# Copies of queries and keys as transfers within SBUF, group scaling on ScalarE, and a deeper early-load pipeline in a two-layer trunk

## The chip, the cores and the metric

The kernel runs on one core of one Trainium2 chip. The metric is the device time of one execution in microseconds (us). Below, PE is the matrix engine, DVE the vector engine, ACT the scalar (activation) engine, POOL the GpSimd engine and SP the engine that here issues almost all DMAs. SBUF is the on-chip working memory of 128 partitions, PSUM the accumulators that PE writes.

## The reference

One batch of 512 tokens with 1024 features goes through two layers, each of the form `x <- x + RMSNorm(mixer(RMSNorm(x)))`. The first layer holds 16 state-space (SSD) heads in 4 groups beside 16 forgetting-attention (FoX) heads; the second is a causal convolution module, which the change does not touch. All is float32. Cut to what matters for the change:

```
u = rmsnorm(x, g_pre);  proj = u @ w_in                       # 7200 columns: z, xBC, dt, q, k, v, f
yg = (y * silu(z_ssd)).reshape(b, s, SSD_GROUPS, 256)
yg = yg * rsqrt(mean(yg * yg, axis=-1) + EPS)                 # one scale per token and group
o: logits = (q . k) * 64**-0.5 + c_t - c_s, causal;  o = softmax(logits) @ v   # 16 heads of 64
out = concat([y, o]) @ w_out
x1 = x + rmsnorm(out, g_post);  then the convolution layer with its own o_w_in and o_w_out
```

## The kernel before, in words

Every large product is made of three PE matmuls on rounded parts: a float32 tensor is split into a high part (a rounded cast, mostly on ACT) and a low part (the difference, on DVE or POOL), and high x high, high x low and low x high are summed in PSUM. So every weight tile that is loaded (512 KB, L163) needs a cast (ACT, L157 or L159) and a subtraction (DVE or POOL, L191).

**Order of the work.** The program is a list of jobs (a weight tile and the matmuls on it), run one after the other. Between the matmuls of the first layer's jobs a small planner (`Steps`) puts the steps of the SSD groups and of the attention heads, each due a set modelled time after the steps that it needs: scores of a head (`sa`) are due 9 modelled us after its queries and keys (`("q", h), 9` and `("k", h), 9`). PE's order is thereby fixed in the program. On DVE, ACT, POOL and SP a scheduler puts the instructions in an order of its own when the program is built; on the chip each of these engines runs its list strictly in order, so an instruction that waits holds back all behind it.

**SSD groups.** For each of 4 groups, `gate` multiplies y by the gate, `gate_sums` takes the sums of squares (ACT, L358) and a power (POOL, L351), `gate_scale` (L1431) scales the four token blocks of 128 x 256, and `to_yT` transposes them on PE. PE transposes the next group's convolved inputs (`x_tokens`, tile `xt`) once their SiLU has run on ACT (tile `cv`, L95), and these need three convolution taps on DVE (L533).

**Queries and keys.** `qk_proj` makes two heads per pair of jobs. For each head the tile QS holds the rounded queries in partitions 0 to 63 (ACT, L610) and their low part in 64 to 127 (DVE, L611); QX repeats the rounded queries in 0 to 63 (L612) and has four rows of ones and cumulated gates below (POOL L613, DMA L614). KS holds the rounded keys (ACT, L623) twice (L625), KX their low part (DVE, L624) and four rows likewise (L626, L627). One score block is then two matmuls, KS x QS and KX x QX.

**Early low parts.** The second layer's weights are large, and DVE is full there. So `lo_ahead` makes the low parts of 52 of its weight tiles while the first layer runs: `load` (L202, 512 KB) brings a tile into SBUF, `sub` casts it into a scratch tile `prh` (ACT, L211, two halves) and subtracts that in place (DVE, L212, two halves), `store` writes the low part to DRAM (L216), from where the second layer fetches it. One step of this generator is taken every 7 or 8 pieces of the job list. In `run` and in the step order of `lo_ahead` a tile's subtraction comes two steps after its load.

Of the kernel before, what the change touches and what calls it, by code (L numbers as in the profile page):

```python
# [9 lines left out]
F32R = mybir.dt.float32r  # L10
BF16 = mybir.dt.bfloat16
AF = mybir.ActivationFunctionType
ALU = mybir.AluOpType
AX = mybir.AxisListType

P = 128
S = 512
# [19 lines left out]
def trunk(  # L37
# [6 lines left out]
    nc = tc.nc  # L44
    V, G, A, T = nc.vector, nc.gpsimd, nc.scalar, nc.tensor
# [2 lines left out]

    cp = ctx.enter_context(tc.tile_pool(name="const", bufs=1))
    rp = ctx.enter_context(tc.tile_pool(name="raw", bufs=3))  # L50
    ep = ctx.enter_context(tc.tile_pool(name="early", bufs=3))
    eh = ctx.enter_context(tc.tile_pool(name="earlyh", bufs=1))
    qp = ctx.enter_context(tc.tile_pool(name="q", bufs=7))
    tp = ctx.enter_context(tc.tile_pool(name="t", bufs=54))
    hp = ctx.enter_context(tc.tile_pool(name="spill", bufs=8, space=bass.MemoryType.DRAM))
    lop = ctx.enter_context(tc.tile_pool(name="los", bufs=64, space=bass.MemoryType.DRAM))
    sp = ctx.enter_context(tc.tile_pool(name="small", bufs=8))
# [11 lines left out]
    def nm(s):  # L69
        uid[0] += 1  # L70
        return f"{s}_{uid[0]}"

    def t2(s, dt=F32):
        return tp.tile([P, S], dt, tag="t", name=nm(s))
# [10 lines left out]
    def f32(t):  # L85
        return t.bitcast(F32)
# [108 lines left out]
    def lo_ahead(js):  # L195


        def load(j):
            w, r0, nk, c0, n = j.spec
            t = ep.tile([P, 1024], F32, tag="e", name=nm("pre"))  # L200
            with tc.issue_after(last_load[0]):
                nc.sync.dma_start(t.rearrange("p (k f) -> p k f", k=nk),  # L202
                                  w[r0 : r0 + nk * P, c0 : c0 + n].rearrange("(k p) f -> p k f", p=P))
            return t

        def sub(t):
            h = eh.tile([P, 1024], F32R, tag="eh", name=nm("prh"))
            for i in range(2):
                sl = slice(i * S, i * S + S)
                with tc.issue_after(last_cast[0]):  # L210
                    A.copy(h[:, sl], t[:, sl])  # L211
                V.tensor_tensor(t.bitcast(F32R)[:, sl], t[:, sl], f32(h)[:, sl], ALU.subtract)  # L212

        def store(j, t):
            j.lo = lop.tile([P, 1024], F32, tag="lo", name=nm("lo"))
            nc.sync.dma_start(j.lo, t)  # L216
        loaded = []
        for i in range(len(js) + 2):
            if i > 1:
                sub(loaded[i - 2])  # L220
            if i > 2:
                store(js[i - 3], loaded[i - 3])
            if i < len(js):
                loaded.append(load(js[i]))
            yield
        store(js[-1], loaded[-1])
# [47 lines left out]
    early = iter(())  # L274
# [243 lines left out]
    def fm_job(w, c0, evac, uh, ul, eng=None):  # L518
        def go(wh, wl):
            pb = bank("m")  # L520
            yield from fm_chunks(pb, P, wh, wl, uh, ul)
            evac(pb)
        return Job(w, 0, KT, c0, P, go, eng)
# [80 lines left out]
    def qk_proj(j):  # L604
        def evac_q(pq):
            for s in range(2):
                h = 2 * j + s
                src = slice(64 * s, 64 * s + 64)
                QS, QX = t2("QS", F32R), t2("QX", F32R)
                A.mul(QS[0:64, :], pq[src, :], 0.125)  # L610
                V.scalar_tensor_tensor(QS[64:128, :], pq[src, :], 0.125, f32(QS)[0:64, :], ALU.mult, ALU.subtract)  # L611
                V.tensor_copy(QX[0:64, :], f32(QS)[0:64, :])  # L612
                G.memset(f32(QX)[64:68, :], 1.0)  # L613
                nc.sync.dma_start(f32(QX)[66:68, :], f32(chl)[32 + h : 33 + h, :, :])  # L614
                qk["q", h] = (QS, QX)
                done["q", h] = now[0]

        def evac_k(pk):
            for s in range(2):
                h = 2 * j + s  # L620
                src = slice(64 * s, 64 * s + 64)
                KS, KX = t2("KS", F32R), t2("KX", F32R)
                A.copy(KS[0:64, :], pk[src, :])  # L623
                V.tensor_tensor(KX[0:64, :], pk[src, :], f32(KS)[0:64, :], ALU.subtract)  # L624
                V.tensor_copy(KS[64:128, :], f32(KS)[0:64, :])  # L625
                G.memset(f32(KX)[64:68, :], 1.0)  # L626
                nc.sync.dma_start(f32(KX)[64:66, :], f32(chl)[64 + h : 65 + h, :, :])  # L627
                qk["k", h] = (KS, KX)
                done["k", h] = now[0]
        fm_job(e_w_in, C_Q + j * P, evac_q, uh, ul)  # L630
        fm_job(e_w_in, C_K + j * P, evac_k, uh, ul)
# [624 lines left out]
    def q256(t, c):  # L1256
        return t[c // 2][:, c % 2 * 256 : c % 2 * 256 + 256]
# [169 lines left out]
    def gate_scale(g):  # L1427
        with tc.high_priority(offset=HP):
            y, r = SG[g]["y"], SG[g]["r"]
            for c in range(NB):  # L1430
                V.tensor_scalar(q256(y, c), q256(y, c), r[:, c : c + 1], None, ALU.mult)  # L1431

    def to_yT(g, f):
        y = SG[g]["y"]
# [14 lines left out]
    def ssd(steps):  # L1449
        add = steps.add  # L1450
        add("tk", decay_chain, ("dt", 24))
        for g in range(4):
# [29 lines left out]
            add(("gate", g), lambda g=g: gate(g), (("ya", 4 * g + 3), 0), (("yo", g), 0), (("silu", g // 2), 0), pe=False)  # L1482
            add(("gq", g), lambda g=g: gate_sums(g), (("gate", g), DL[9]), pe=False)
            add(("gs", g), lambda g=g: gate_scale(g), (("gq", g), DL[10]), pe=False)
            for f in range(2):
                add(("yT", g, f), lambda g=g, f=f: to_yT(g, f), *([(("yT", g, 0), 0)] if f else [(("gs", g), DL[11])]))
# [72 lines left out]
    for j in jobs[6:40]:  # L1559
        j.eng = G  # L1560
    early = lo_ahead([j for j in jobs[J1:JO1] + jobs[JO1 + 4 : JO1 + 8] if not j.make])
    run(1)
    steps = Steps()
# [30 lines left out]
    for half in range(2):  # L1594
        sl = slice(half * 256, half * 256 + 256)
# [51 lines left out]
```

## Time and profile before

| | us |
|---|---|
| median of 3 runs (927.5 to 927.8) | 927.53 |
| profiled execution, its own time | 929.48 |
| its span, first to last instruction | 927.6 |
| PE busy | 892.8 (96%) |
| DVE busy | 740.6 (80%) |
| ACT busy | 604.5 (65%) |
| POOL busy | 520.6 (56%) |

All rows are of the profiled execution. "Idle before" is the time for which the engine did nothing ahead of an instruction, with the instruction that ended that wait. The first layer fills the span up to about 570 us, the second the rest. SP, which only issues DMAs, has no busy time in these views.

### The profile page before, as it was taken

Reading aid. Unit: us, or ns where it says so; the run is one execution under the profiler, and the core shown is the slowest. Engines: PE = TensorE matmul, PEld = TensorE weight load, DVE = VectorE, ACT = ScalarE, POOL = GpSimd, SP = SyncE. Lnnn points to the kernel's source line nnn. Section 1 sums busy time; section 2 is a strip of 40 time slices with the busy share of each in tenths; the row PEclk is TensorE's granted clock in tenths of the full one; section 3 lists DMA queues with packets and bytes.
Section 4 is the critical chain, followed back from the end, with each engine's and each line's share of the span. In section 5 each row is a group of like instructions: output and inputs, shape, how many; then the busy total and the mean of one; then the engine's idle time right before and its main releaser. Section 6 shows DMA issues by size and latency. Waiting matters only on the chain.

```text
span 927.6 us, 13837 instructions
## 1 busy us (share of the span) xinstructions
PE 892.8 (96%) x4603; PEld 748.1 (81%) x4603; DVE 740.6 (80%) x1318; ACT 604.5 (65%) x1143; POOL 520.6 (56%) x478
## 2 busy tenths in 40 slices
PE   6999999997999999989899999999999999999997
PEld 6888788886888888778678889888888887787885
DVE  5667979888888897988888437899999999979502
ACT  5767567566856676577686437788785968658300
POOL 2733665554543444335573202998999999847410
PEclk9999999998999999999999999999999999999999
DMA  6736523348764675664648993655664655544503
GB/s 208 231 105 209 154 69 91 91 125 254 235 212 153 192 242 160 195 215 150 215 157 285 341 344 106 199 161 180 201 208 136 214 194 160 166 153 155 185 1 113
DMA packets 182506, 166.12 MB, mean 179 GB/s; under 512 B 7900, under 2 KB 151908, under 8 KB 182436
## 3 DMA queue, kind: packets, MB, share of 16 engines
q1 hardware_dynamic: 182420, 165.25, 55.6%
q8 instruction: 36, 0.59, 0.3%
q14 instruction: 34, 0.28, 0.1%
q10 hardware_dynamic: 16, 0.00, 0.0%
HBM read 133.64 MB, written 31.46 MB: 178 GB/s over the span
## 4 chain that ended last, share of the span: by engine, by line
PE 64%; DVE 14%; ACT 7%; issue 6%; DMA 4%; POOL 3%; SPq 0%; DVEq 0%; POOLq 0%; ACTq 0%
PE m L102 37%; PE o L102 18%; PE tm L102 4%; DVE pre L212 3%; POOL w L191 2%; ACT w L159 1%; DMA lo<-pre 1%; DMA pre<-in_o_w_in_dram 1%; PE s L102 1%; PE pT L106 1%; DVE cv L533 1%; DVE y L1431 1%; DVE seg L1380 1%; DVE pl L119 1%; DVE w L191 1%
## 5 line engine op out<-in xcount | busy, mean ns | idle before, releaser
L102 PE MATMUL m<-uh,w 128*128 128x512 f32 (+1 forms) x1392 | 452.9, 392 | 1.7 <-ACT yT L1441 1.0
L102 PEld LDWEIGHTS m<-uh,w 128*128 128x128 f32 x1392 | 261.9, 190 | 50.7 <-ACT yT L1441 1.4
L102 PE MATMUL m<-ul,w 128*128 128x512 f32 (+1 forms) x696 | 268.0, 385 | 0.0
L191 POOL TENSOR_TENSOR w<-wr,w 128x512 fp32r<-128x512 f32 x112 | 168.1, 1526 | 148.3 <-ACT w L159 112.3
L989 DVE SCALAR_TENSOR_TENSOR acc<-h,cw,acc 128x490 f32<-128x490 f32 (+13 forms) x274 | 178.9, 727 | 2.7 <-ACT acc L981 2.0
L896 POOL TENSOR_TENSOR acc<-acc,prod 128x507 f32<-128x507 f32 (+9 forms) x124 | 159.6, 1289 | 8.2 <-ACT prod L882 0.7
L102 PEld LDWEIGHTS m<-ul,w 128*128 128x128 f32 x696 | 132.4, 190 | 21.8 <-issue 0.5
L102 PE MATMUL o<-w,hlh 128*128 128x512 f32 x448 | 140.2, 394 | 0.8 <-ACT pr L95 0.8
L212 DVE TENSOR_TENSOR pre<-pre,prh 128x512 fp32r<-128x512 f32 x104 | 92.3, 906 | 29.1 <-ACT prh L211 28.9
L102 PEld LDWEIGHTS o<-w,hlh 128*128 128x128 f32 x448 | 82.4, 188 | 16.7 <-ACT pr L95 0.9
L102 PE MATMUL tm<-w,uh 128*128 128x256 f32 (+1 forms) x384 | 92.5, 332 | 1.3 <-DVE QS L611 1.0
L1509 POOL TENSOR_SCALAR pr<-pr,ri 128x128 f32<-128x128 f32 (+1 forms) x64 | 40.0, 626 | 92.6 <-DVE ri L1508 79.8
L102 PE MATMUL o<-w,hll 128*128 128x512 f32 x224 | 87.5, 391 | 0.5 <-POOL hll L119 0.5
L159 ACT CAST w<-wr 128x1024 fp32r<-128x1024 f32 x72 | 74.9, 1050 | 20.1 <-DMA wr<-in_e_w_in_dram 7.7
L211 ACT CAST prh<-pre 128x512 fp32r<-128x512 f32 x104 | 61.0, 620 | 41.0 <-DVE pre L212 15.6
L882 ACT ACTIVATE prod<-h,cw 128x507 f32<-128x507 f32 (+9 forms) x124 | 79.1, 710 | 0.0
L351 POOL TENSOR_TENSOR rstd<-var,mhalf 128x1 f32<-128x1 f32 (+1 forms) x20 | 12.9, 644 | 105.5 <-DVE var L349 80.0
L157 ACT CAST w<-wr 128x1024 fp32r<-128x1024 f32 x56 | 57.3, 1051 | 18.5 <-DMA wr<-in_o_w_out_dram 10.4
L102 PEld LDWEIGHTS tm<-w,uh 128*128 128x128 f32 x384 | 64.0, 193 | 6.4 <-DVE QS L611 1.1
L102 PE MATMUL tm<-w,ul 128*128 128x256 f32 (+1 forms) x192 | 61.7, 322 | 0.0
L95 ACT ACTIVATE pr<-s,nmx 128x128 f32<-128x128 f32 (+1 forms) x64 | 33.9, 530 | 36.4 <-DVE nmx L1503 29.3
L102 PEld LDWEIGHTS o<-w,hll 128*128 128x128 f32 x224 | 42.0, 188 | 10.3 <-POOL hll L119 0.9
(267 smaller groups left out, 1564.6 us busy)
## 6 DMA issues: line engine op xcount, KB each, us to landing
wr<-in_e_w_in_dram SPq DMA_DIRECT2D x56, 512.0 KB
lo<-pre SPq DMA_DIRECT2D x52, 512.0 KB
pre<-in_o_w_in_dram SPq DMA_DIRECT2D x48, 512.0 KB
wr<-in_o_w_in_dram SPq DMA_DIRECT2D x48, 512.0 KB
w<-lo SPq DMA_DIRECT2D x48, 512.0 KB
wr<-in_e_w_out_dram SPq DMA_DIRECT2D x16, 512.0 KB
wr<-in_o_w_out_dram SPq DMA_DIRECT2D x16, 512.0 KB
x<-in_x_dram SPq DMA_DIRECT2D x12, 256.0 KB
```

The costliest lines, as they stand in the source:

```text
L95: i = A.activation(*a, **kw)
L102: T.matmul(o, l, r, start=start, stop=stop, skip_group_check=True)
L157: last_cast[0] = A.copy(hi, src).ins
L159: last_cast[0] = A.copy(hi, src).ins
L191: j.eng.tensor_tensor(hl[1][i][:, sl], src[:, sl], f32(hl[0][i])[:, sl], ALU.subtract)
L211: A.copy(h[:, sl], t[:, sl])
L212: V.tensor_tensor(t.bitcast(F32R)[:, sl], t[:, sl], f32(h)[:, sl], ALU.subtract)
L351: mark["rstd"] = G.tensor_tensor(r, v, mhalf.to_broadcast([P, ss.shape[-1]]), ALU.pow).ins
L882: A.activation(prs[i][:, s:], hs[j][:, : S - s], AF.Copy, scale=w31(30 - s, j))
L896: G.tensor_tensor(a2[j][:, s:], a2[j][:, s:], prs.pop(i)[:, s:], ALU.add)
L989: V.scalar_tensor_tensor(a[:, s:], h[:, : S - s], w31(30 - s, j), a[:, s:], ALU.mult, ALU.add)
L1509: G.tensor_scalar(p[:, :L], p[:, :L], ri, 1.0, ALU.mult, ALU.mult)
```

## The change

Four edits, all in the first layer's stretch. (1) The second copies of the rounded queries (QX rows 0 to 63) and of the rounded keys (KS rows 64 to 127) are no longer DVE copies but DMAs from SBUF to SBUF of 64 x 512 float32 (128 KB) on SP's queue, 32 in all. (2) The 16 scalings of `gate_scale` are ACT activations instead of DVE instructions. (3) The scratch tile of the early low parts is two tiles of half the size instead of one, the pool of early tiles has four instead of three, and the general pool `t` has 52 tiles instead of 54. (4) A tile's subtraction comes three steps after its load, not two, and its store one step after that.

```diff
-    ep = ctx.enter_context(tc.tile_pool(name="early", bufs=3))
-    eh = ctx.enter_context(tc.tile_pool(name="earlyh", bufs=1))
+    ep = ctx.enter_context(tc.tile_pool(name="early", bufs=4))
+    eh = ctx.enter_context(tc.tile_pool(name="earlyh", bufs=2))
-    tp = ctx.enter_context(tc.tile_pool(name="t", bufs=54))
+    tp = ctx.enter_context(tc.tile_pool(name="t", bufs=52))
...
         def sub(t):
-            h = eh.tile([P, 1024], F32R, tag="eh", name=nm("prh"))
             for i in range(2):
+                h = eh.tile([P, S], F32R, tag="eh", name=nm("prh"))
                 sl = slice(i * S, i * S + S)
                 with tc.issue_after(last_cast[0]):
-                    A.copy(h[:, sl], t[:, sl])
-                V.tensor_tensor(t.bitcast(F32R)[:, sl], t[:, sl], f32(h)[:, sl], ALU.subtract)
+                    A.copy(h, t[:, sl])
+                V.tensor_tensor(t.bitcast(F32R)[:, sl], t[:, sl], f32(h), ALU.subtract)
...
-        for i in range(len(js) + 2):
-            if i > 1:
-                sub(loaded[i - 2])
+        for i in range(len(js) + 3):
             if i > 2:
-                store(js[i - 3], loaded[i - 3])
+                sub(loaded[i - 3])
+            if i > 3:
+                store(js[i - 4], loaded[i - 4])
             if i < len(js):
                 loaded.append(load(js[i]))
...
-                V.tensor_copy(QX[0:64, :], f32(QS)[0:64, :])
+                nc.sync.dma_start(f32(QX)[0:64, :], f32(QS)[0:64, :])
...
-                V.tensor_copy(KS[64:128, :], f32(KS)[0:64, :])
+                nc.sync.dma_start(f32(KS)[64:128, :], f32(KS)[0:64, :])
...
-                V.tensor_scalar(q256(y, c), q256(y, c), r[:, c : c + 1], None, ALU.mult)
+                A.activation(q256(y, c), q256(y, c), AF.Copy, scale=r[:, c : c + 1])
```

PE's order is the same in both programs. The order of DVE, ACT and SP moves at many places; three of them follow. The first is DVE's list at the scaling of the third SSD group (`y`), between the taps of two convolved tiles (`cv`), before:

```order
L533 SCALAR_TENSOR_TENSOR cv_2207<-m_2148,c_136,cv_2207 128x510
L347 TENSOR_SCALAR var_2231<-ss_2222 128x4
L533 SCALAR_TENSOR_TENSOR cv_2207<-m_2148,c_136,cv_2207 128x509
L1431 TENSOR_SCALAR y_1797<-y_1797,rstd_2233 128x256 x2
L1431 TENSOR_SCALAR y_1818<-y_1818,rstd_2233 128x256 x2
L212 TENSOR_TENSOR pre_2291<-pre_2291,prh_2394 128x512 x2
L533 SCALAR_TENSOR_TENSOR cv_2269<-m_2212,c_136,cv_2269 128x511
L533 SCALAR_TENSOR_TENSOR cv_2269<-m_2212,c_136,cv_2269 128x510
L533 SCALAR_TENSOR_TENSOR cv_2269<-m_2212,c_136,cv_2269 128x509
```

The same place of DVE's list in the changed program (buffer numbers differ):

```order
L533 SCALAR_TENSOR_TENSOR cv_2206<-m_2146,c_136,cv_2206 128x510
L347 TENSOR_SCALAR var_2230<-ss_2221 128x4
L533 SCALAR_TENSOR_TENSOR cv_2206<-m_2146,c_136,cv_2206 128x509
L212 TENSOR_TENSOR pre_2292<-pre_2292,prh_2498 128x512
L533 SCALAR_TENSOR_TENSOR cv_2269<-m_2211,c_136,cv_2269 128x511
L533 SCALAR_TENSOR_TENSOR cv_2269<-m_2211,c_136,cv_2269 128x510
L533 SCALAR_TENSOR_TENSOR cv_2269<-m_2211,c_136,cv_2269 128x509
L212 TENSOR_TENSOR pre_2292<-pre_2292,prh_2501 128x512
```

Between the two convolved tiles stood four scalings and two early subtractions; now one early subtraction stands there.

ACT's list at the same place before, from the last sum of squares (`junk`) to the SiLU of the second convolved tile:

```order
L358 ACTIVATE junk_2229,ss_2222<-y_1818 128x256
L159 CAST w_2427<-wr_2282 128x1024
L211 CAST prh_2394<-pre_2291 128x512
L95 ACTIVATE cv_2207<-cv_2207 128x512
L211 CAST prh_2394<-pre_2291 128x512
L531 ACTIVATE cv_2269<-m_2212,c_135,c_136 128x512
L118 CAST hlh_2309<-cv_2085 128x512
L159 CAST w_2524<-wr_2345 128x1024
L118 CAST hlh_2313<-cv_2143 128x512
L211 CAST prh_2495<-pre_2333 128x512 x2
L95 ACTIVATE cv_2269<-cv_2269 128x512
```

And ACT's list there in the changed program, from the weight cast on:

```order
L159 CAST w_2430<-wr_2282 128x1024
L1431 ACTIVATE y_1795<-y_1795,rstd_2232 128x256 x2
L1431 ACTIVATE y_1816<-y_1816,rstd_2232 128x256 x2
L95 ACTIVATE cv_2206<-cv_2206 128x512
L211 CAST prh_2498<-pre_2292 128x512
L531 ACTIVATE cv_2269<-m_2211,c_135,c_136 128x512
L118 CAST hlh_2310<-cv_2083 128x512
L159 CAST w_2528<-wr_2347 128x1024
L118 CAST hlh_2314<-cv_2141 128x512
L211 CAST prh_2501<-pre_2292 128x512
L211 CAST prh_2564<-pre_2335 128x512
L95 ACTIVATE cv_2269<-cv_2269 128x512
```

The four scalings stand between the weight cast and the first SiLU, where they wait for POOL's `rstd`; an early cast in front of that SiLU is gone.

The third place is SP's list around the keys of heads 4 and 5 before (`chl` are the cumulated gates, `lo` and `pre` the early stores and loads, `wr` the weight loads):

```order
L216 DMA lo_3627<-pre_3306 128x1024
L163 DMA wr_3706<-in_e_w_in_dram 128x8x128
L202 DMA pre_3629<-in_o_w_in_dram 128x8x128
L216 DMA lo_3680<-pre_3413 128x1024
L627 DMA KX_3588<-chl 2x1x512
L627 DMA KX_3595<-chl 2x1x512
L202 DMA pre_3682<-in_o_w_in_dram 128x8x128
```

The same place of SP's list in the changed program:

```order
L216 DMA lo_3644<-pre_3208 128x1024
L163 DMA wr_3724<-in_e_w_in_dram 128x8x128
L202 DMA pre_3646<-in_o_w_in_dram 128x8x128
L216 DMA lo_3698<-pre_3320 128x1024
L625 DMA KS_3603<-KS_3603 64x512
L627 DMA KX_3604<-chl 2x1x512
L216 DMA lo_3811<-pre_3428 128x1024
L625 DMA KS_3610<-KS_3610 64x512
L627 DMA KX_3611<-chl 2x1x512
L202 DMA pre_3700<-in_o_w_in_dram 128x8x128
```

The key copies are beside the small `chl` transfers that were there already; the second of them stands behind one more early store.

## Rows read from the trace of the kernel before

**Rows 1.** Page: busy us (share of the span) xinstructions.

```profile
PE 892.8 (96%) x4603; PEld 748.1 (81%) x4603; DVE 740.6 (80%) x1318; ACT 604.5 (65%) x1143; POOL 520.6 (56%) x478
```

**Rows 2.** Stretches: length, busy PE, PEld, DVE, ACT, POOL, PE clock, DMA share, GB/s.

```profile
200.00:225.00 25.00, 22.16 (x105) 17.92 (x103) 24.07 (x33) 13.45 (x28) 12.31 (x10) 1.00 0.74 232
225.00:250.00 25.00, 22.26 (x111) 19.10 (x112) 19.50 (x41) 19.18 (x33) 10.66 (x7) 0.86 0.88 273
...
375.00:400.00 25.00, 22.91 (x139) 18.99 (x138) 22.75 (x43) 17.27 (x37) 10.44 (x15) 1.00 0.69 219
400.00:425.00 25.00, 23.18 (x147) 20.24 (x145) 17.68 (x42) 16.59 (x43) 9.61 (x14) 0.93 0.53 180
425.00:450.00 25.00, 24.13 (x126) 19.15 (x124) 23.00 (x39) 16.31 (x34) 12.18 (x14) 1.00 0.50 172
450.00:475.00 25.00, 21.69 (x113) 15.76 (x113) 22.00 (x49) 20.02 (x51) 17.93 (x21) 1.00 0.68 228
...
600.00:625.00 25.00, 25.00 (x112) 20.70 (x111) 24.79 (x47) 19.96 (x31) 23.08 (x21) 1.00 0.55 169
```

**Rows 3.** Waits of PE: us in total, times, longest us.

```profile
PE xt L106 <- ACT cv L95: 4.0, 1, 4.0
...
PE yd L102 <- DVE hll L119: 1.9, 2, 1.0
PE yT L106 <- DVE y L1431: 1.5, 2, 0.9
```

**Rows 4.** Timeline of DVE, ACT and PE, 216 to 228: start us, us, instruction.

```profile
216.12 5.25 DVE L1431 TENSOR_SCALAR y<-y,rstd 128x256 f32<-128x256 f32 x4 [0.41 <-POOL rstd L351]
221.29 3.45 DVE L212 TENSOR_TENSOR pre<-pre,prh 128x512 fp32r<-128x512 f32 x2
224.66 2.31 DVE L533 SCALAR_TENSOR_TENSOR cv<-m,c,cv 128x511 f32<-128x511 f32 x3
...
218.29 1.05 ACT L159 CAST w<-wr 128x1024 fp32r<-128x1024 f32 x1
...
227.06 0.63 ACT L95 ACTIVATE cv<-cv 128x512 f32<-128x512 f32 x1 [1.15 <-DVE cv L533]
...
227.74 0.90 PE L106 MATMUL xt<-ident,cv 128*128 128x128 f32 x3 [4.04 <-ACT cv L95]
```

**Rows 5.** Line L1431, ns min/median/max; and one ACT pass of that size.

```profile
L1431 DVE TENSOR_SCALAR y<-y,rstd x16: 341/1374/1386, 119.3 to 277.6; 128x256 f32<-128x256 f32 x16
...
213.00 0.40 ACT L358 ACTIVATE junk<-y 128x256 f32<-128x256 f32 x1
```

**Rows 6.** Tiles QX and KS, ns min/median/max, first and last start us.

```profile
L612 DVE CAST QX<-QS x16: 414/420/1399, 281.3 to 445.4; 64x512 fp32r<-64x512 f32 x16
...
L625 DVE CAST KS<-KS x16: 420/422/1066, 284.9 to 459.5; 64x512 fp32r<-64x512 f32 x16
```

**Rows 7.** Timeline of ACT, DVE and PE at two stalls among the heads.

```profile
400.96 0.62 ACT L211 CAST prh<-pre 128x512 fp32r<-128x512 f32 x1 [1.48 <-DMA pre<-in_o_w_in_dram]
403.10 0.50 PE L102 MATMUL s<-KS,QS 128*128 128x512 f32 x1 [1.82 <-ACT pr L95]
...
446.23 0.67 DVE L212 TENSOR_TENSOR pre<-pre,prh 128x512 fp32r<-128x512 f32 x1
446.98 0.62 ACT L211 CAST prh<-pre 128x512 fp32r<-128x512 f32 x1 [1.85 <-issue]
448.13 0.72 PE L102 MATMUL o<-w,hlh 128*128 128x512 f32 x2 [0.80 <-ACT pr L95]
```

**Rows 8.** Chain of waits: start us, us, a DMA from issue to landing.

```profile
74.28 2.49 DMA lo<-pre
```

**Rows 9.** Waits of SP's queue: us in total, times, longest us.

```profile
SPq L202 <- DMA lo<-pre: 72.9, 35, 5.8
```

**Rows 10.** Timeline of ACT and PE, head 4: rounded keys, then first scores.

```profile
326.58 0.57 ACT L623 CAST KS<-m 64x512 fp32r<-64x512 f32 x1
331.72 0.22 PE L102 MATMUL s<-KS,QS 128*128 128x128 f32 x1
```

## The prediction

> **What bounds the kernel now.** I read the page first: PE is busy for 892.8 of 927.6 us [rows 1], and its order and number of matmuls are the same after the change. So the change can only win back time in which PE stands still or runs slowly. The table of stretches shows where: PE's idle time is the length of a stretch less its busy time, 2.84 us at 200 to 225, 2.74 at 225 to 250, and 2.09, 1.82, 0.87 and 3.31 (together 8.09) from 375 to 475 [rows 2]. In the second layer it is none: at 600 to 625 PE is busy for all 25.00 us although DVE is busy for 24.79 [rows 2]. The same rows show two dips of the granted clock, a mean of 0.86 at 225 to 250 and 0.93 at 400 to 425, where the levels are 1 and 0.5 (2.4 and 1.2 GHz): 0.14 x 25 / 0.5 = 7.0 us and 3.5 us at the lower level, of which a busy PE loses half, 3.5 and 1.75. Both stand behind idle time of PE: 4.04 us before 227.74 [rows 4], 1.82 us before 403.10 [rows 7].
>
> Then the list of PE's waits, for who ends them: `xt` for the SiLU on ACT 4.0, `yd` for DVE 1.9, `yT` for the scaling on DVE 1.5 [rows 3]. Last the timelines of DVE, ACT and POOL ahead of these waits, because DVE, at 22 to 24 of 25 us in most of these stretches [rows 2], is the engine with a backlog.
>
> **Part 1, the scalings.** At 216 the four scalings hold DVE for 5.25 us, then two early subtractions for 3.45, then three taps for 2.31; the SiLU starts at 227.06 and PE's `xt` at 227.74 after 4.04 idle [rows 4]. In the new DVE list one early subtraction is left between the taps. The next tap then waits for ACT, whose list in front of the last SiLU is four scalings, a SiLU, seven other passes. One scaling there I price at 0.40, the pass over the same tile [rows 5]: four are 1.6, and with the first SiLU (0.63) and the seven passes (six at the 0.62 of an early cast [rows 7], an estimate, and a weight cast of 1.05 [rows 4], together 4.8) ACT reaches the last SiLU at 216.1 + 1.6 + 0.6 + 4.8 = 223.1 and ends it at 223.7 instead of 227.7. PE would want it at 223.7 less the 1.5 of `yT` waits, which the ACT scaling (done at 217.7, against 221.4) ends: 222.2. So some 1.5 of stall stay. Saved: 1.5 + (4.0 - 1.5) = 4.0. With the stall little over a third as long I take the dip as gone or halved: of its 3.5, minus the idle at its edge, I count 2.7. Part 1: 6.7. Bounds: 0 (another early cast holds ACT) and 1.5 + 4.0 + 3.5 = 9.0.
>
> At the other three groups the same four instructions leave DVE (1.37 each by the median [rows 5]), but PE waits for `yT` in only two places [rows 3], so I count nothing there; ACT, at 13 to 20 of 25 us [rows 2], has room for 1.6.
>
> **Part 2, the copies.** 32 DVE copies go, 16 for QX at a median of 0.420 and 16 for KS at 0.422 [rows 6]: 13.5 us at least, and more where they run up to 1.4. They lie between 281 and 460 [rows 6], some 8% of that stretch. In their place SP issues 32 transfers of 128 KB. None of these is in the trace. Nearest is the early store, 512 KB from SBUF to DRAM, 2.49 from issue to landing [rows 8]; below, the 0.42 of the copy; above, a transfer that stands behind an early load waiting up to 5.8 for an earlier store [rows 9], 8.3 in all. I take 2.5, the nearest row. The Trainium skill ("DMA: Bandwidth & Descriptors", section "Anatomy of one DMA — SWDGE (gpsimd) path") prices a transfer of another queue at a fixed 2.0 us and 436 GB/s, by which 128 KB would take an estimated 2.3: it speaks against this edit, as no transfer, however small, would be as quick as the DVE copy, and by it the sum would be the same. The copy must land before the head's first scores. For head 4 the rounded keys end at 327.15 and the scores start at 331.72, a slack of 4.57 [rows 10]; that hides 2.5 and the delay of an early store in front, but not 8.3. Were every cover gone, each late head would cost PE up to 8.3 - 4.57 = 3.7. I price the copies at 1.5 lost in all (bounds 0 and 18.5, for which I assume that five of the 16 heads are as tight as head 4). A late weight load behind a waiting copy on SP's queue falls under the same bounds.
>
> **Part 3, the early loads.** ACT runs in order, so an early cast that waits holds back the exponentials behind it. At 400.96 it waited 1.48 for its load, and PE then stood 1.82 [rows 7]; a load one step earlier has 7 or 8 pieces of the job list more to land. At 446.98 it waited 1.85 for nothing that the profile names; DVE's subtraction of the tile before, from the one scratch tile, ended at 446.90, and PE stood 0.80 [rows 7]. With two half tiles the cast waits only for the subtraction before the last. So parts 2 and 3 work on the same 8.09 of idle and the same dip of 1.75. The DVE list shows that some of the freed time is filled with early subtractions brought forward, 104 in all as before, so I take two thirds of the 9.8: 6.5. Bounds: 0 and 9.8. The two waits of `yd` (1.9) lie where subtractions are placed anew: half, 1.0. Two tiles fewer in pool `t`, I price at nothing: no wait of PE above ends with a tile that comes free; if that cover fails, a stall of the size of the largest here, 4.0, is the price.
>
> **The sum.** -6.7 - 6.5 - 1.0 + 1.5 = -12.7. The profiled execution took 929.48 for a span of 927.6, so 916.8 for one like it; it lies 1.95 above the median of the runs, 927.53, against which the forecast is 927.5 - 12.7 = 914.8, in round numbers 914.5. Its own range is 909 to 920.
>
> **The rivals.**
> *Only the scaling pays.* The freed time among the heads is taken up by early subtractions that the scheduler pulls in front of the maxima, and the idle there stays. For: there is no less of them in all. Against: the waits in rows 7 are of early casts, which have more room now. -6.7 - 1.0 + 1.5 = -6.2: 921.
>
> *Nearly all stalls go.* All of part 1 (9.0), of the 9.8 and of `yd` (1.9): -20.7, 907. For: DVE falls by 16 x 1.37 + 13.5 = 35 us of 740.6. Against: each engine still runs in order, and the chain of a score block passes ACT, DVE and POOL whatever DVE does elsewhere.
>
> *The change doesn't do what it says.* ACT becomes late at `xt` in DVE's place (its list there holds the scalings in front of the SiLU), so part 1 shrinks to the 1.5 of `yT`, the heads win 2 and lose as much to the copies: 926 to 928, no change. For: ACT's path above is only 4 us shorter than DVE's was. Against: that path carries no wait that the trace shows.
>
> *Slower by the copies.* SP runs in order, and a key copy behind a load that waits up to 5.8 for a store [rows 9] lands after its scores are due. At 3.7 a head, five heads give +18.5 - 6.7 - 6.5 - 1.0 = +4.3, and two new dips like the one of 3.5 us, 1.75 each, bring 7.8: 932 to 935. It decides from about four late heads on. For: there are 35 such waits [rows 9], and the new list puts a store in front of head 5's copy. Against: the small transfers on the same queue, just as placed, are in no row of PE's waits.
>
> **Chances.** Forecast (909 to 920) 0.52; only the scaling (920 to 925.7) 0.17; nearly all (below 909) 0.12; no change 0.07; slower 0.12. What can be told from no change is 0.2%, 1.9 us. Faster is 0.52 + 0.17 + 0.12 = 0.81, same 0.07, slower 0.12. The range for 8 in 10 goes from 905, past the full gain, to 928, past no change, and leaves out the slower case and the last of the gains.
>
> **What would show it.** Part 1: no idle over 1.5 us of PE before the third group's `xt`, `yT` gone from PE's waits, the granted clock near 1.00 there, and the scaling on ACT near 0.4. Part 2: DVE's busy time lower by 30 to 35; no `s` of PE that waits for a DMA. Part 3: ACT's early casts wait less for DVE, for loads and for "issue", and PE's idle at 375 to 475 falls to some 3. Waits of `s` for DMA KS or QX over 2 us, or SP standing long in front of L612 and L625, would make the forecast wrong; so would a new stall at ACT's scaling for POOL's `rstd`.

## The result: 918.0 us, and the profile after

The changed kernel takes 917.98 us (median of 4 runs, 916.27 to 919.47) against 927.66 of the kernel before (4 runs beside it): a ratio of 0.9895, 95% interval 0.9881 to 0.9909, or 9.7 us less. A second set on another chip gave 0.9889 (0.9868 to 0.9910). The forecast was 914.5 with a range of 905 to 928. Of the two profiled executions the later took 917.41 against 929.48, 12.1 less; the one of before lay 1.95 above its median, so the traces below show some 2 us more than the medians do.

The page's engine line (columns as in [rows 1]):

```profile
PE 888.8 (97%) x4603; PEld 747.9 (82%) x4603; DVE 711.5 (78%) x1270; ACT 613.2 (67%) x1159; POOL 508.7 (56%) x478
```

DVE has lost 29.1 us of work, and PE's idle time has fallen from 34.8 to 26.8 us. The table of stretches shows where, and one thing that the forecast didn't have (columns as in [rows 2]):

```profile
200.00:225.00 25.00, 23.87 (x116) 19.64 (x116) 21.49 (x31) 18.15 (x36) 13.22 (x10) 1.00 0.74 230
225.00:250.00 25.00, 23.36 (x150) 21.13 (x149) 24.57 (x44) 20.58 (x36) 14.45 (x10) 0.98 0.76 244
250.00:275.00 25.00, 25.00 (x128) 22.24 (x128) 20.07 (x36) 15.86 (x34) 9.74 (x11) 0.89 0.81 263
...
375.00:400.00 25.00, 23.63 (x170) 21.05 (x169) 20.88 (x44) 17.14 (x43) 11.43 (x17) 1.00 0.81 248
400.00:425.00 25.00, 25.00 (x141) 20.49 (x141) 18.93 (x38) 18.20 (x40) 8.47 (x14) 1.00 0.57 188
425.00:450.00 25.00, 22.72 (x113) 17.70 (x113) 20.39 (x40) 18.45 (x43) 14.83 (x18) 0.93 0.72 221
450.00:475.00 25.00, 23.73 (x132) 18.57 (x131) 20.22 (x39) 20.32 (x45) 17.81 (x19) 1.00 0.64 212
```

PE's idle time from 375 to 475 is 1.37 + 0.00 + 2.28 + 1.27 = 4.92 us, against 8.09 [rows 2]. (The program runs 7 to 13 us ahead by then, so these stretches hold later work; between the same matmuls the idle time falls from 8.08 to 3.90.) The granted clock is 1.00 at 200 to 225 now, but 0.89 at 250 to 275, where it was 1.00 before: PE is busy there for all 25.00 us and loses by its clock alone. The dips of 225 to 250 and 400 to 425 [rows 2] have not gone, they stand some 20 and 35 us later, and their time at the 0.5 level is about 10 us in all, as before: (0.02 + 0.11 + 0.07) x 25 / 0.5.

PE's waits, the lines that answer to [rows 3] and the new ones among the larger:

```profile
PE yd L102 <- DVE hll L119: 1.4, 3, 0.9
PE yd L102 <- DVE H L1346: 1.4, 1, 1.4
PE pT L106 <- ACT pr L95: 1.3, 1, 1.3
PE pT L106 <- DVE pl L119: 1.2, 2, 0.9
PE xt L106 <- ACT cv L95: 1.1, 1, 1.1
```

`yT` is gone and `xt` is 1.1 instead of 4.0. `yd` has a second row that was there before with 0.7 (for H, the state of an SSD group, updated in L1346); its two rows had 2.6 together and have 2.8 now. No wait for a transfer to KS or QX is among PE's waits. The timelines of ACT and PE at the third group, which answer to [rows 4]:

```profile
213.85 1.71 ACT L1431 ACTIVATE y<-y,rstd 128x256 f32<-128x256 f32 x4 [1.36 <-POOL rstd L351]
...
220.19 0.63 ACT L95 ACTIVATE cv<-cv 128x512 f32<-128x512 f32 x1
...
220.87 0.55 PE L106 MATMUL xt<-ident,cv 128*128 128x128 f32 x3 [1.13 <-ACT cv L95]
```

The line of the scaling, which answers to [rows 5] (ns min/median/max):

```profile
L1431 ACT ACTIVATE y<-y,rstd x16: 492/496/513, 118.8 to 266.9; 128x256 f32<-128x256 f32 x16
```

Four scalings take 1.71 on ACT, 0.43 each as they overlap, and ACT reaches the last SiLU with 1.13 of PE's stall left. ACT waits 1.36 for POOL's `rstd` ahead of them. From there to the SiLU at 220.19 ACT has no idle time, and DVE's taps for that SiLU start only behind ACT's L531 among them, at 217.31. So this wait stands in the chain that ends in PE's 1.13; how much of it that is, no run shows.

**Where the time went, by place in the program.** PE's 4603 matmuls are the same in the same order in every kernel here. So the list can be cut at the matmuls that start at 200, 217, 236, 262, 290, 375 and 475 us in the kernel before, and the time from cut to cut compared, whatever the reason (idle or clock). Worked out from the starts of PE's matmuls in the profiled executions, in us, as differences from the kernel before; "scale", "copies" and "early" are the three edits, each kernel named by what it has of them:

```
cut at            0     217     236     262     290     375     475     all
before (us)   214.9    19.0    25.9    28.1    85.1   100.0   446.1
scale          -1.7    -7.9    +5.7    -0.5    -0.7    +0.1    -0.4    -5.4
copies         +0.7    -0.9    +0.7    +2.4    -0.9    -7.8    +0.1    -5.8
early          +0.4    -0.5    -0.8    -0.4    +2.4    -2.3    +1.9    +0.6
scale, early   -1.1    -7.8    +2.7    -0.5    +1.2    -1.0    +0.4    -6.1
copies, early  +5.2    -5.0    -0.8    -0.2    -0.2    -5.1    +0.7    -5.3
scale, copies  -2.0    -8.3    +5.5    -0.5    -0.6    -8.4    +0.1   -14.1
  once more    -2.5    -8.3    +5.9    -0.4    -0.4    -8.9    +0.1   -14.5
all three      -2.0    -7.7    +4.3    -0.5    -1.0    -6.4    +1.0   -12.3
  once more    -2.5    -7.7    +5.7    -0.5    -1.0    -6.2    +0.9   -11.3
```

Each row is one profiled execution, so it also holds where that execution's clock fell: two profiles of the same kernel differ by up to 1.4 in a column. The +5.2 and -5.0 of "copies, early" are of that kind. That execution, the slowest of the kernel's six, spent about 10 us at the 0.5 level from 193 us on, where no other did; PE so came later to `xt` and waited 2.2 there instead of 4.0.

Three things stand in the table. The scalings win 8 us at the third group's `xt` (column 217) and give back 3 to 6 in the column behind it. Most of the gain among the heads (column 375) comes with the copies, in every company; the early loads bring 2.3 there when alone and take 2 to 3 away when the copies are there. And behind 475, where the second layer follows, no kernel gains more than 0.4.

### The profile page after: what moved, and what is told of

It reads as the page before. It is cut to its first block, busy times and chain, and to the rows that moved or that the text cites. A ratio compares the mean times of both kernels' runs of the same rounds, so it can differ in the third digit from the quotient of the medians.

```text
span 915.6 us, 13920 instructions
## 1 busy us (share of the span) xinstructions
PE 888.8 (97%) x4603; PEld 747.9 (82%) x4603; DVE 711.5 (78%) x1270; ACT 613.2 (67%) x1159; POOL 508.7 (56%) x478
## 5 line engine op out<-in xcount | busy, mean ns | idle before, releaser
L191 POOL TENSOR_TENSOR w<-wr,w 128x512 fp32r<-128x512 f32 x112 | 159.2, 1446 | 141.9 <-ACT w L159 104.6
L1509 POOL TENSOR_SCALAR pr<-pr,ri 128x128 f32<-128x128 f32 (+1 forms) x64 | 39.7, 621 | 85.6 <-DVE ri L1508 61.8
```

The source lines that it names most:

```text
L191: j.eng.tensor_tensor(hl[1][i][:, sl], src[:, sl], f32(hl[0][i])[:, sl], ALU.subtract)
L1509: G.tensor_scalar(p[:, :L], p[:, :L], ri, 1.0, ALU.mult, ALU.mult)
```

## The experiments

Each kernel was timed beside runs of the kernel before on one chip (medians there 927.7 to 930.0). In one table:

| kernel | median us | ratio to before | 95% interval |
|---|---|---|---|
| scale only | 924.94 | 0.9950 | 0.9935 to 0.9965 |
| copies only | 923.40 | 0.9936 | 0.9920 to 0.9951 |
| early only | 930.16 | 1.0005 | 0.9992 to 1.0018 |
| scale and early | 923.33 | 0.9939 | 0.9921 to 0.9958 |
| copies and early | 923.02 | 0.9933 | 0.9915 to 0.9950 |
| scale and copies | 916.28 | 0.9868 | 0.9850 to 0.9886 |
| scale and copies, once more | 917.21 | 0.9881 | 0.9860 to 0.9902 |
| all three (the change) | 917.98 | 0.9895 | 0.9881 to 0.9909 |
| all three, once more | 918.77 | 0.9889 | 0.9868 to 0.9910 |

**The scalings alone.**

```diff
-                V.tensor_scalar(q256(y, c), q256(y, c), r[:, c : c + 1], None, ALU.mult)
+                A.activation(q256(y, c), q256(y, c), AF.Copy, scale=r[:, c : c + 1])
```

> The kernel before, with only L1431 moved from DVE to ACT. Theory (the scalings earn the two waits at the third group and no more, and the stretch at half clock only moves to the next pause of PE): the wait for `yT` (1.5) goes and the one for `xt` falls from 4.0 to about 1, so -4 to -4.5: 923 to 923.5, with as many us at the 0.5 level as before (10.2), in other places. Rival of the prediction (the half clock behind `xt` goes as well): -6.7, 921, and some 3.4 to 6.8 us at the 0.5 level instead of 10.2. Second rival (what pays in the changed kernel is that DVE and POOL get free, and the scalings are most of it): -7 or more, 920 or below, and PE's idle time at 375 to 475 falls as well.

Measured: -4.6 (0.9950; by the interval -3.2 to -6.0), at the edge of the first theory; the rival's -6.7 is out. Its sign was seen all the same: the time at the 0.5 level fell from 10.2 to 6.8 us (3.4 in each of two dips). The wait for `yT` did go and that for `xt` fell to 0.9, but a new one stands behind them. The timelines of ACT and PE in this kernel's trace:

```profile
235.13 1.14 ACT L211 CAST prh<-pre 128x512 fp32r<-128x512 f32 x2 [4.96 <-DMA pre<-in_o_w_in_dram]
236.17 0.58 ACT L600 COPY zf<-m 128x512 f32<-128x512 f32 x1
236.80 0.69 PE L102 MATMUL m<-uh,w 128*128 128x512 f32 x1 [4.66 <-ACT zf L600]
```

and its stretch, with a dip behind the new stall:

```profile
225.00:250.00 25.00, 20.34 (x114) 17.50 (x112) 20.34 (x39) 19.15 (x34) 13.36 (x10) 0.93 0.80 249
```

ACT, ahead of its old pace, reaches an early cast whose load hasn't landed, waits 4.96, and the eviction L600 behind it holds a PSUM bank that PE needs. PE runs into the next late thing as soon as the first is gone. Below, this is the wait for `m`.

**The copies alone.**

```diff
-                V.tensor_copy(QX[0:64, :], f32(QS)[0:64, :])
+                nc.sync.dma_start(f32(QX)[0:64, :], f32(QS)[0:64, :])
...
-                V.tensor_copy(KS[64:128, :], f32(KS)[0:64, :])
+                nc.sync.dma_start(f32(KS)[64:128, :], f32(KS)[0:64, :])
```

> The kernel before, with only the 32 copies of L612 and L625 made by transfers that SP issues. Theory: DVE's busy time falls by some 15 to 20 us, PE's idle time at 375 to 475 (8.1) by 1 to 3, and no `s` waits for a transfer, since one lands 2 to 5 us after its issue: -1 to -3, 925 to 926.5. Rival (the copies carry the gain among the heads): -5 or more, 922.5 or below. Rival (a transfer is later than the DVE copy and costs where the slack is small): 0 to +2, with waits of `s` for a transfer to KS or QX.

Measured: -5.9 (0.9936), the rival by which the copies carry the gain among the heads: PE's idle time at 375 to 475 falls from 8.09 to 3.15, and the table's column there by 7.8. It also shows what a late transfer costs. SP and PE at the first head:

```profile
284.90 0.35 SPq L216 DMA_DIRECT2D lo<-pre  x1
285.31 0.48 SPq L625 DMA_DIRECT2D KS<-KS  x1
...
288.21 0.30 PE L102 MATMUL s<-KS,QS 128*128 128x128 f32 x1 [2.50 <-DMA KS<-KS]
```

The transfer is issued right behind an early store and the scores start 2.90 after its issue, 2.50 late.

**The early loads alone.** The third part of the change (4 tiles `pre`, two half tiles `prh`, three steps, 52 tiles in pool `t`), without the others.

```diff
-    ep = ctx.enter_context(tc.tile_pool(name="early", bufs=3))
-    eh = ctx.enter_context(tc.tile_pool(name="earlyh", bufs=1))
+    ep = ctx.enter_context(tc.tile_pool(name="early", bufs=4))
+    eh = ctx.enter_context(tc.tile_pool(name="earlyh", bufs=2))
...
-        for i in range(len(js) + 2):
+        for i in range(len(js) + 3):
...
```

> The kernel before, with only the early loads three steps ahead (4 tiles `pre`, 2 half tiles `prh`, 52 tiles in pool `t`). Theory: idle time of ACT in front of its early casts falls from 41 to about 17 us as in the changed kernel, and PE's idle time at 375 to 475 from 8.1 to 5 or 6: -2 to -4, 923.5 to 925.5. Rival (the casts wait because DVE is behind, and it stays so without the other two edits): -1 to +1, and ACT's idle time there stays above 30 us. Rival (these loads are the gain among the heads by themselves): -6, 921.5.

Measured: 1.0005, no change, the first rival. ACT's waits ahead of early casts in this kernel (us in total, times, longest us):

```profile
ACT prh L211 <- DVE pre L212: 24.8, 24, 3.6
ACT prh L211 <- DVE yo L1369: 3.1, 1, 3.1
ACT prh L211 <- DMA pre<-in_o_w_in_dram: 1.8, 1, 1.8
```

and in the kernel with the copies alone:

```profile
ACT prh L211 <- DVE pre L212: 15.6, 9, 4.8
ACT prh L211 <- DMA pre<-in_o_w_in_dram: 10.1, 6, 3.7
ACT prh L211 <- DVE y L1417: 4.2, 1, 4.2
ACT prh L211 <- issue: 2.9, 2, 1.7
ACT prh L211 <- DMA pre<-in_o_w_out_dram: 2.7, 1, 2.7
```

With the early loads the waits for loads are nearly gone (1.8), and instead ACT waits longer for DVE's subtractions, 29.7 in all: the rival's reason, just under the 30 that it named. The totals are of the whole span. At the two stalls of [rows 7] themselves the early loads alone did help: PE's 1.82 became 0.67, now for DVE, and the 0.80 became 0.36.

```profile
401.64 0.50 PE L102 MATMUL s<-KS,QS 128*128 128x512 f32 x1 [0.67 <-DVE pl L119]
```

But new waits of 0.86 and 0.81, for POOL's scaling of the exponentials (L1509), came right behind, and the heads' idle time fell only from 8.08 to 6.08. With the copies alone the same two matmuls wait 0.11 and 0.00, the heads' idle time is 3.14, and ACT's early casts still wait there, 1.4 for loads. So what the early loads take away, the late load and the scratch tile, was the smaller part of what held PE. That the rest was DVE's backlog is argued from the copies' gain and not shown by itself: the copies also change the order of ACT's list there.

**The change less one part.** First without the copies, then without the scalings (the lines of the two diffs above, undone in the changed kernel).

> The changed kernel with the 32 copies of L612 and L625 back on DVE; the scalings stay on ACT and the early loads three steps ahead. The difference from the changed kernel (918.0) is the copies' share when the rest is there. Theory: 919 to 921, the copies are worth 1 to 3. Rival (the copies cost as much as they free, as they land 2 to 5 us after their issue): 917 to 918.5. Rival (DVE's backlog among the heads is what they take away): 923 or more.

> The changed kernel with the scalings of L1431 back on DVE; the copies stay transfers and the early loads three steps ahead. Alone, against the kernel before, the scalings gave -4.6 (ratio 0.995), the copies -5.9 (0.9936), the early loads 0 (1.0005). Theory (the copies are the gain among the heads, and the early loads add nothing to them): -5 to -7, ratio 0.9925 to 0.995, with `xt` at 4.0 and `yT` among PE's waits again, and PE's idle time at 375 to 475 about 3 to 5. Rival of the prediction (early loads and copies share a gain of about 6.5 and the loads carry part of it, by about 2 beyond the copies): -8, 0.991.

Measured: 0.9939 and 0.9933. Taking the copies out of the change costs 0.0044 x 928 = 4.1, more than the theory's 1 to 3 and less than the 5 of the rival with DVE's backlog (PE idle at 375 to 475: 7.09 without them, 4.92 with). Taking the scalings out costs 3.5, and the early loads add 0.0003 to the copies, nothing.

**Without the early loads.** The kernel before with the lines of the first two diffs.

> The kernel before with the scalings on ACT and the copies as transfers, the early loads as they were (3 whole tiles `pre`, one `prh`, two steps, 54 tiles in pool `t`). Theory (the early loads are worth nothing alone, but cover the scalings: without them one early cast waits for its load and holds back L600, and PE stood 4.7 for `m` when the scalings were moved alone): -6 to -8, ratio 0.9915 to 0.9935, with that wait of about 4.7 again, 2 to 3 us slower than the changed kernel. Rival (the early loads are worth nothing in any company): -9 to -11, as fast as the changed kernel or faster, and no such wait.

Measured: -12.3 (0.9868). Both theories miss: it is as fast as the changed kernel or faster, although the wait for `m` is there:

```profile
PE m L102 <- ACT zf L600: 4.6, 1, 4.6
```

So that wait, which the early loads do remove, isn't worth its length. In the column at 236 PE has 4.64 us of idle time here and 3.4 at the 0.5 level; in the two profiles of the changed kernel it has 1.6 of idle time, but 6.8 and 10.2 at the 0.5 level. Run once more, to see whether the chips tell these apart:

> The scalings on ACT and the copies as transfers, the early loads and the 54 tiles of pool `t` as before, run once more: this version measured 0.9868 of the kernel before, the changed kernel 0.9895 and 0.9889, the same version with 52 tiles 0.9898, each beside its own runs of the kernel before. Theory (the third part costs something, mostly through its two tiles and a longer stretch at half clock): 0.985 to 0.988 again, the stall of 4 to 5 for `m` and one stretch of about 3.4 us at the 0.5 level behind it. Rival (the four are one and the same within what the chips scatter): 0.9885 or above.

> The changed kernel as it is, run beside the next ones on one chip, because the 2.6 between it and the run without the early loads was measured on different chips. Theory (the third part costs something in the company of the other two): ratio to before 0.988 to 0.991, as before. Rival (the difference lay in the chip): 0.9865 or below, like the run without the early loads.

Measured: 0.9881, between theory and rival, with a wait of 4.9 and 3.4 us at the 0.5 level as the theory said, and 0.9889, within the theory. On average the version without the early loads stands 0.0018, or 1.6 us, below the changed kernel, and the intervals overlap: the early loads bring nothing, and that they cost something is likely but not shown.

**Half of the third part.** Scalings and copies, and of the third part the two half tiles alone: with two steps, 3 tiles `pre` and 54 tiles in `t`.

```diff
-    eh = ctx.enter_context(tc.tile_pool(name="earlyh", bufs=1))
+    eh = ctx.enter_context(tc.tile_pool(name="earlyh", bufs=2))
...
```

> The changed kernel with the early loads two steps ahead as before (3 tiles `pre`, 54 tiles in pool `t`), but with the two half tiles `prh`. It tells which half of the third part covers the scalings: the third step of lead, or the scratch in halves. Theory (the lead: it is the load that is late): like the run without the third part, -6 to -8, with a wait of `m` for `zf` over 3 us. Rival (the halves: early casts that wait less for DVE issue earlier everywhere): as fast as the changed kernel, -9 to -11, without that wait.

Measured: 917.73, 0.9873 (0.9854 to 0.9892), with a wait of 4.2 for `m`. So the wait isn't removed by the halves; the lead with its fourth tile is left, as the theory said. The time is the rival's.

**The two tiles.** Scalings, copies and this:

```diff
-    tp = ctx.enter_context(tc.tile_pool(name="t", bufs=54))
+    tp = ctx.enter_context(tc.tile_pool(name="t", bufs=52))
```

> The kernel before with the scalings on ACT and the copies as transfers, and 52 tiles in pool `t` instead of 54; the early loads stay as before. It tells whether the two tiles that the third part takes from the pool cost what it loses. Theory (the prediction's price of nothing was right): ratio 0.986 to 0.988, as with 54 tiles. Rival (the pool is what costs): 0.989 to 0.991, with new waits of PE among the heads.

Measured: 919.68, 0.9898 (0.9877 to 0.9919), the rival's value, but the interval reaches into that of 54 tiles. By the times alone this is inconclusive. In the trace the column at 375 is 2.6 to 3.1 us longer than with 54 tiles (-5.8 against -8.4 and -8.9), part of it a dip:

```profile
375.00:400.00 25.00, 23.50 (x149) 20.59 (x148) 19.98 (x41) 17.60 (x40) 10.97 (x15) 0.93 0.78 237
```

The other kernels go the same way. With the copies issued once, the five profiles with 54 tiles win 7.8 to 8.9 in that column (-8.7 in the run with the half tiles, -8.3 in the next one), and the four with 52 tiles win 5.1 to 6.4, with the early loads or without; none of the five has a dip of the clock there, and each of the four has. So the two tiles probably cost some 2.5 us among the heads. How they do it stays open: the waits are others here than in the changed kernel, and no run has the full early loads with 54 tiles.

**The stall for `m` taken away in another way.** Scalings, copies, and one eviction on DVE, which has room there:

```diff
-            A.copy(oT[j], pb)
+            (V.tensor_copy if j == 1 else A.copy)(oT[j], pb)
```

> The kernel before with the scalings on ACT, the copies as transfers, and one eviction of L600 (j = 1, the one that stands behind the waiting early cast on ACT) on DVE instead; the early loads stay as before. Theory (the 4.6 that PE stands for `m` come from ACT's order alone, and a bank that DVE empties is free before 231): the wait goes and of the 4.6 two to four are won: -2 to -4 against the run without the edit, ratio 0.9825 to 0.985, faster than the changed kernel by 5 to 7. Rival (PE next needs what ACT makes behind the same cast, `hlh` of `Bt` and of `xe`): the stall moves there, 0 to -1, ratio 0.986 to 0.987. Second rival (the bank comes free no earlier on DVE): no change.

Measured: 921.29, 0.9910 (0.9889 to 0.9931): slower than without the edit, which no theory had. The stretches of 5 us of the version without the edit, where PE's stall is 4.64:

```profile
230.00:235.00 5.00, 0.51 (x3) 0.07 (x1) 1.97 (x4) 1.53 (x4) 0.82 (x1) 0.99 1.10 360
235.00:240.00 5.00, 4.86 (x15) 3.90 (x16) 4.50 (x16) 4.97 (x10) 2.99 (x2) 0.67 0.70 224
240.00:245.00 5.00, 5.00 (x34) 4.57 (x33) 5.00 (x9) 4.97 (x8) 3.47 (x2) 1.00 0.55 178
```

The timeline of PE with the edit, its three longer waits there:

```profile
232.54 0.47 PE L102 MATMUL m<-uh,w 128*128 128x512 f32 x1 [0.92 <-DVE y L1303]
240.17 0.39 PE L102 MATMUL st<-hll,hlh 128*128 128x256 f32 x1 [0.71 <-POOL hll L119]
246.65 0.30 PE L102 MATMUL yd<-xd,hll 128*128 128x64 f32 x1 [1.51 <-DVE hll L119]
```

and its stretches of 5 us behind them:

```profile
245.00:250.00 5.00, 3.02 (x20) 2.74 (x20) 5.00 (x5) 4.99 (x8) 2.73 (x2) 0.87 0.27 67
250.00:255.00 5.00, 5.00 (x25) 5.00 (x25) 4.44 (x8) 3.25 (x8) 2.70 (x2) 0.50 0.28 83
255.00:260.00 5.00, 5.00 (x25) 5.00 (x25) 4.64 (x10) 3.46 (x6) 2.54 (x2) 0.50 0.65 218
260.00:265.00 5.00, 5.00 (x35) 5.00 (x34) 4.29 (x8) 1.68 (x4) 0.86 (x1) 0.76 0.98 326
```

The one long stall is gone and three shorter ones take its place (0.92, 0.71, 1.51; a fourth is 0.47). PE now reaches DVE's and POOL's work earlier, and DVE has the eviction to do besides; the run doesn't tell the two apart. Then PE runs at the 0.5 level: with the long stall 0.33 x 5 / 0.5 = 3.3 us, here (0.13 + 0.50 + 0.50 + 0.24) x 5 / 0.5 = 13.7 us, of which a busy PE loses half, 1.7 and 6.9. What the shorter idle time won (1.0), the clock took back, and more. It wasn't this one execution: the mean granted clock is 0.991 to 0.993 in five of the six runs and 0.996 in the fastest (918.43), against 0.995 to 0.998 in the eight runs without the edit.

**The transfers doubled.** In the changed kernel each copy is issued twice.

```diff
                 nc.sync.dma_start(f32(QX)[0:64, :], f32(QS)[0:64, :])
+                nc.sync.dma_start(f32(QX)[0:64, :], f32(QS)[0:64, :])
...
                 nc.sync.dma_start(f32(KS)[64:128, :], f32(KS)[0:64, :])
+                nc.sync.dma_start(f32(KS)[64:128, :], f32(KS)[0:64, :])
```

> The changed kernel with each of the 32 transfers of L612 and L625 issued twice, the second right behind the first into the same rows; nothing else differs. It prices the lateness of a copy, since the data are there only after the second. Theory (a copy lands 2.2 to 4.7 us after its issue and the smallest slack to the head's scores is 1.0, 1.8, 2.4, 2.5): with 2 to 3 us more, four to six heads wait 0.5 to 2 us each, +3 to +7 against the changed kernel, and PE's list of waits has `s` for the transfer of KS or QX. Rival (slack is there at most heads and SP has room): 0 to +1.5, with one such wait at most.

Measured: 930.70, 1.0011 (0.9988 to 1.0034), 11 us slower than the changed kernel and above both theories. One line of PE's waits has most of it:

```profile
PE s L102 <- DMA KS<-KS: 10.7, 3, 5.6
```

Three late heads cost 10.7 of idle time, 3.6 each, and more than the whole gain of the change is gone. It hangs on these transfers landing in time.

## Why the prediction was right, and where it was not

The time (918.0 against 914.5) and the side were right. By the prediction's own terms:

- **Part 1, the stalls (4.0): right.** `yT` 1.5 gone, `xt` 4.04 to 1.13 instead of the 1.5 foreseen; the scaling 0.43 for a price of 0.40. At its place the part even brought 7.7, dip included. POOL's `rstd`, which the prediction named as a sign against it, did hold ACT there for 1.36, in the chain that ends in the remaining 1.13.
- **Part 1, the dip (2.7): the term that was mis-sized.** "With the stall little over a third as long I take the dip as gone or halved" held at 227 and nowhere else. In the changed kernel PE stops for 1.35 at 247 (for L1346 on DVE, which is busy for 24.57 of 25 us there), and the clock is at 0.5 right behind it: 4.3 us given back between the cuts at 236 and 262, 5.7 in the second profile. The time at the 0.5 level is about 10 us before and after, and 14 in the second profile, so the term brought nothing, or cost up to 1.7. Part 1 alone measured -4.6 where 6.7 were written.
- **Parts 2 and 3, the heads (6.5 less 1.5 for the copies, 5.0 net): near in sum (6.4 in the column at 375), wrong in cause.** The prediction read a late load and a late scratch tile out of [rows 7] and counted on the lead and the halves. The runs show that the copies do more without them (7.8), that the early loads alone bring 2.3 there and nothing in all, and that with all three the heads get back about 2 us less than with two.
- **The copies' price (1.5): more than was paid here**, as no head waits in the changed kernel; with the copies alone one head lost 2.5. The rival "slower" had the price of a late head right, 3.7 against 3.6 with the transfers doubled, where three late heads were enough to eat the gain; the prediction had it decide from about four.
- **`yd` (1.0): not there in sum.** The waits for DVE's `hll` fell from 1.9 to 1.4, as foreseen by half; the one for H, which the prediction left out, grew from 0.7 to 1.4.
- **The other groups ("I count nothing there"): 0.9 missed.** With the scalings alone PE gains 1.5 between 160 and 195 us; its wait of 0.95 at 191, for an eviction of `yT` (L1441), is 0.2 there. In the changed kernel that wait is still 0.8, and the gain is 0.9.
- **Two tiles at nothing: probably mis-sized**, by some 2.5 us among the heads, as the kernels with 52 and with 54 tiles show side by side.

Of the signs it named, `yT` gone, no `s` behind a DMA, and fewer ACT waits were seen; DVE's fall (29.1) was just short of 30, PE's idle time among the heads 4.92 (3.90 between the same matmuls) instead of some 3, and "the granted clock near 1.00 there" was true of 200 to 225 only. "Nearly all stalls go" failed because new waits appear, "only the scaling pays" because the copies do.

That the sum came so near is in part luck. In the profiles the change wins 12.3 and 11.3 by place against the 12.7 of the sum, because too much for the dip and for `yd` stands against too little for the heads and nothing for the other groups. By the medians it wins 9.7; most of this last difference is that the profile before, from which the gains were priced, was of an execution 1.95 slower than its median.

No version here is shown to beat the changed kernel; scalings and copies alone, two of its edits left out, are at least as fast (916.3 and 917.2 against 918.0 and 918.8).

## What to carry to other kernels

A stall removed brings its own idle time at its place, but look further for the next thing that is late, since PE gets there earlier (it stood 15 us behind the first with the scalings alone, 27 us in the changed kernel); a dip of the clock behind a stall is no gain to count until the stretch behind is free of stalls as well. When two edits share a gain, ask which engine's work the bottleneck waits for: less work on the engine with the backlog paid here, an earlier load for an engine that waited did little. A copy that leaves a busy engine for a DMA queue is worth it while every landing has slack, so price a late one before relying on it.

## What the runs showed of the hardware that was not expected

- The time at the lower of the clock's two levels didn't follow the idle time ahead of it: 3.3 us at 0.5 behind one stall of 4.64, 13.7 behind stalls of 0.92, 0.71 and 1.51 in a kernel that differs by one eviction. Nor did the same pause bring the same dip. PE's stall of about 1.35 for H (L1346) near 248 us was followed by no time at 0.5 with the transfers doubled, 3.4 us in the change without the copies, 6.8 in the changed kernel and 10.2 in its second profile. In this order, the stretches behind it:

```profile
250.00:255.00 5.00, 5.00 (x44) 5.00 (x44) 5.00 (x13) 3.29 (x7) 0.01 (x1) 1.00 0.64 210
250.00:255.00 5.00, 5.00 (x35) 5.00 (x35) 5.00 (x12) 3.58 (x7) 0.60 (x1) 0.76 0.65 212
250.00:255.00 5.00, 5.00 (x25) 5.00 (x25) 5.00 (x11) 4.16 (x7) 1.39 (x1) 0.50 0.64 216
250.00:255.00 5.00, 5.00 (x26) 5.00 (x25) 5.00 (x12) 4.05 (x7) 1.07 (x1) 0.50 0.67 216
```

The runs of one kernel differ too: the changed kernel had a mean granted clock of 0.996 and a span of 914.5 in one run, 0.992 and 917.7 in another. The Trainium skill ("TensorE: Matmul & The Clock Gate", section "Part 1: The HAM clock gate") says that the monitor isn't reset by a kernel's start, and that the moment at which the clock changes varies with it; these rows are in line with that, but no run here tests it.
- A 128 KB transfer within SBUF, 64 rows of 2 KB, was waited for until 2.90 us after its issue, where the DVE copy takes 0.42 [rows 6]. Two issued one behind the other made PE wait up to 5.6.
